# Two products against the same weights joined into one of 512 columns in the late feed-forward blocks of a decoder layer

## Chip, cores and metric

The kernel runs on one core of one Trainium2 chip. The metric is the device time of one execution in microseconds (us). The kernel before was run three times; the median is 517.9 us (517.75 to 518.09).

## What is computed

The reference is one decoder layer over 256 tokens of 1024 channels, in float32. Two token mixers (a gated linear recurrence and a block-sparse attention) read the same input, are projected, gated, merged and normalised. What the change touches comes behind that: the feed-forward part, with D_FF = 2816.

```python
x = layer_norm(DN_ALPHA * x + mixed, ln1_w, ln1_b)      # called x1 in the kernel
h = jnp.einsum('bsd,df->bsf', x, w_ffn_in)              # 1024 -> 2 * 2816
h_gate, h_up = jnp.split(h, 2, axis=-1)
y = jnp.einsum('bsf,fd->bsd', jax.nn.silu(h_gate) * h_up, w_ffn_down)
return layer_norm(DN_ALPHA * x + y, ln2_w, ln2_b)
```

## The kernel before, in words

**Three products for one.** TensorE is fed with a rounded format (fp32r). To keep float32 accuracy each operand is split into leading bits and a rest: `split` (L135) lets ScalarE copy the value into the rounded format (L136) and VectorE subtract that copy from the value (L137). A product a·w is then the sum of three: ah·wh, al·wh and ah·wl, accumulated in the same PSUM area.

**Weights.** `plan` (L71) lists all weight tiles of 1 MB in the order of their use. `stage` (L143) loads one tile over SyncE's queue (SP, L158) into one of three raw buffers (pool wraw), ScalarE casts it to wh (L159) and VectorE subtracts to get wl (L161); wh and wl have four buffers each (pools whi and wlo). `fetch` (L165) hands out the next tile and keeps up to three more staged ahead.

**Blocks of the feed-forward part.** A tile of w_ffn_in has 8 steps k (128 input channels each) of 256 output columns, so two blocks f of 128 features. `feat_pair` (L205) takes one tile, one PSUM bank `[128, 2, 256]` of the pool mm, and calls `feat_steps` (L213) for f = 0 and 1. There the weights are the stationary operand, 128 x 128, and the 256 tokens are the moving one: for each k three products of 256 columns (L217: wh with the leading bits, L218: wh with the rest, L219: wl with the leading bits). Each product loads its own weights into the array.

**x1** is normalised token half by token half (`norm1`), transposed on TensorE (L595) and split into x1h and x1l, two tiles of 8 KB per partition from the pool big (12 slots). The first EARLY = 4 feature blocks are done another way (`FfnEarly`, L599): there x1 is stationary and the weights move. The order of the instructions of TensorE, VectorE and ScalarE is written out by hand up to L665 (`manual_schedule`); behind it a scheduler with a cost model orders the instructions of each engine at build time, in program order where nothing speaks for another.

**The late loop**, j = 4, 6, ... 20 (L670 to L677), nine iterations: a gate tile (name fg) and an up tile (fu), each with `feat_pair`; ScalarE takes Silu of the gate bank (L674), VectorE multiplies with the up bank (L675), and `split` writes two blocks of ah and al, which the down projection reads.

**The down projection** (L679 to L691) has five PSUM parts: two of 512 columns for the first token half, and 512, 256 and 256 for the second. The first four come from the pool aux, the last from mm. Each pool has four banks. aux is not used in the late loop before, except for the last transposes of the early blocks (tile fet, L628).

Of the kernel before, what the change touches and what calls it, by code (L numbers as in the profile page):

```python
# [10 lines left out]
F32 = mybir.dt.float32  # L11
F32R = mybir.dt.float32r
U32 = mybir.dt.uint32
AF = mybir.ActivationFunctionType
# [3 lines left out]
P = 128  # L18
T = 256
NT = T // P  # L20
D = 1024
KC = D // P
# [88 lines left out]
def hybrid_layer_kernel(ctx: ExitStack, tc, x, xT, vecs, wts, ln1_w, ln1_b, ln2_w, ln2_b, consts, out):  # L111
    nc = tc.nc
# [6 lines left out]
    sm = pool("sm", 2)  # L119
    klp = pool("klp", 1)  # L120
    mm = pool("mm", 4, space=PSUM)
    aux = pool("aux", 4, space=PSUM)

    def slot(name, dt=F32):
        return big.tile([P, 2048], dt, tag="s8", name=name)

    def r32(ap):
        return ap.bitcast(F32)


    loads = plan()
# [3 lines left out]
    def split(dst_h, dst_l, src):  # L135
        nc.scalar.copy(dst_h, src)  # L136
        nc.vector.tensor_sub(dst_l, src, r32(dst_h))  # L137
# [5 lines left out]
    def stage(pieces=None, eng=nc.vector):  # L143
        i = state["next"]
        if i >= len(loads):
            return
        state["next"] += 1
        _, _, k, _, _, held = loads[i]
        src = wts[i].rearrange("p (k c) -> p k c", k=k)
        view = lambda z: z.rearrange("p (k c) -> p k c", k=k)  # L150
        raw = view(wraw.tile([P, 2048], F32, tag="raw", name=f"raw{i}"))
        if held:
            h, l = view(slot(f"wh{i}", F32R)), view(slot(f"wl{i}", F32R))
        else:
            h = view(whi.tile([P, 2048], F32R, tag="h", name=f"wh{i}"))
            l = view(wlo.tile([P, 2048], F32R, tag="l", name=f"wl{i}"))
        for ks in ks_of(pieces or (k,)):
            nc.sync.dma_start(raw[:, ks, :], src[:, ks, :])  # L158
            nc.scalar.copy(h[:, ks, :], raw[:, ks, :])  # L159
            yield  # L160
            eng.tensor_sub(l[:, ks, :], raw[:, ks, :], r32(h[:, ks, :]))  # L161
            yield
        ready.append((h, l))

    def fetch(ahead=LOOKAHEAD):  # L165
        while state["next"] < len(loads) and len(ready) < 1 + ahead:
            list(stage())
        return ready.pop(0)
# [36 lines left out]
    def feat_pair(name, ah=None, al=None):  # L205
        ah, al = (xTh, xTl) if ah is None else (ah, al)
        wh, wl = fetch()
        ps = mm.tile([P, 2, T], F32, tag="mm", name=name)
        for f in range(2):
            feat_steps(ps[:, f, :], wh, wl, f, ah, al, range(KC))  # L210
        return ps

    def feat_steps(ps, wh, wl, f, ah, al, ks, k0=0):  # L213
        wcol = slice(f * P, (f + 1) * P)
        for k in ks:
            kk = k0 + k
            nc.tensor.matmul(ps, wh[:, k, wcol], ah[:, kk, :], start=(kk == 0), stop=False)  # L217
            nc.tensor.matmul(ps, wh[:, k, wcol], al[:, kk, :], start=False, stop=False)  # L218
            nc.tensor.matmul(ps, wl[:, k, wcol], ah[:, kk, :], start=False, stop=(kk == KC - 1))  # L219
# [62 lines left out]
    for j in range(2, 4):  # L282
        ps = feat_pair(f"hf{j}")
# [4 lines left out]
    for j in range(4):  # L288
        ps = feat_pair(f"hq{j}")
        sg = sm.tile([P, 2, T], F32, tag="sg", name=f"sgq{j}")  # L290
# [23 lines left out]
    def hgrn_steps():  # L314
# [5 lines left out]
        nc.vector.tensor_mul(kq, flat(Kt), flat(Qg))  # L320
        nc.scalar.copy(kqh, kq)
        nc.vector.tensor_sub(kql, kq, r32(kqh))
        for g in range(4):
            ps = aux.tile([P, 4, P], F32, tag="aux", name=f"sd{g}")
# [73 lines left out]
    class Steps:  # L398
        def __init__(self):
            self.gens = []  # L400
# [21 lines left out]
    for j in range(4):  # L422
        ps = feat_pair(f"hg{j}")
        sg = sm.tile([P, 2, T], F32, tag="sg", name=f"sgg{j}")
# [90 lines left out]
    for j in range(4):  # L515
        side.step()
        ps = feat_pair(f"za{j}", yah, yal)
# [5 lines left out]
    for j in range(4):  # L523
        ps = feat_pair(f"zb{j}", ybh, ybl)
# [45 lines left out]
    def row_parts(name, widths, n0=0):  # L570
        parts = []
        for i, (p, w) in enumerate(widths):
            parts.append((p.tile([P, w], F32, tag="aux" if p is aux else "mm", name=f"{name}{i}"), n0))
            n0 += w
        return parts
# [2 lines left out]
    nc.gpsimd.dma_start(xr, x.rearrange("(t p) d -> p t d", p=P))  # L578
    wb1 = bcast("wb1", ln1_w, ln1_b)
    x1 = slot("x1").rearrange("p (t d) -> p t d", t=NT)  # L580
    x1h = slot("x1h", F32R).rearrange("p (k t) -> p k t", k=KC)
    x1l = slot("x1l", F32R).rearrange("p (k t) -> p k t", k=KC)
    ah = [slot(f"ah{i}", F32R).rearrange("p (k t) -> p k t", k=KC) for i in range(3)]
    al = [slot(f"al{i}", F32R).rearrange("p (k t) -> p k t", k=KC) for i in range(3)]

# [3 lines left out]
    def norm1_transpose(t):  # L589
        ts = slice(t * P, (t + 1) * P)  # L590
        for g in range(2):
            ps = mm.tile([P, 4, P], F32, tag="mm", name=f"x1t{t}{g}")
            for a in range(4):
                k = 4 * g + a
                nc.tensor.transpose(ps[:, a, :], x1[:, t, k * P:(k + 1) * P], ident)  # L595
            ks = slice(4 * g, 4 * g + 4)
            split(x1h[:, ks, ts], x1l[:, ks, ts], ps)

    class FfnEarly:  # L599

# [6 lines left out]
        def product(self, i, w):  # L607
            (wh, wl), ps, ts = w, self.ps[:, i, :], self.ts
            for k in range(KC):
                nc.tensor.matmul(ps, x1h[:, k, ts], wh[:, k, :], start=(k == 0), stop=False)  # L610
                nc.tensor.matmul(ps, x1l[:, k, ts], wh[:, k, :], start=False, stop=False)
                nc.tensor.matmul(ps, x1h[:, k, ts], wl[:, k, :], start=False, stop=(k == KC - 1))

        def gate(self):
            self.product(0, self.wg)
# [17 lines left out]
    pss = [row_parts(f"wo{t}", [(aux, 512)] * 2) for t in range(NT)]  # L633
    wb2 = bcast("wb2", ln2_w, ln2_b)
    with tc.manual_schedule(engines={ET.PE, ET.DVE, ET.Activation}):
# [5 lines left out]
        for q in range(4):  # L641
            if q == 3:
                norm1_transpose(0)
            rows_pass(pss[1], lhs, 1, tiles[q:q + 1], KC)
            if q < 2:
                prefetch(1)
# [5 lines left out]
        e[0][0].silu()  # L652
        e[0][1].gate()
        norm1_transpose(1)
        prefetch(2)
        e[0][1].up()
# [10 lines left out]
    e[1][1].transpose()  # L667


    for j in range(EARLY, NF, 2):  # L670
        pg = feat_pair(f"fg{j}", x1h, x1l)
        pu = feat_pair(f"fu{j}", x1h, x1l)
        sg = sm.tile([P, 2, T], F32, tag="sg", name=f"sf{j}")
        nc.scalar.activation(sg, pg, AF.Silu)  # L674
        nc.vector.tensor_mul(sg, sg, pu)  # L675
        i, k = divmod(j, KC)
        split(ah[i][:, k:k + 2, :], al[i][:, k:k + 2, :], sg)  # L677

    pss = [row_parts("wd0", [(aux, 512)] * 2), row_parts("wd1", [(aux, 512), (aux, 256), (mm, 256)])]  # L679
    lhs = (lambda kk: ah[kk // KC][:, kk % KC, :], lambda kk: al[kk // KC][:, kk % KC, :])  # L680
# [43 lines left out]
```

## Time and profile before

| | before |
|---|---|
| median of 3 runs | 517.9 us (517.75 to 518.09) |
| profiled execution, its own time | 517.71 us |
| its span, first to last instruction | 515.7 us |
| granted TensorE clock, mean | 0.997 |
| late loop (first fg product to first wd product) | 343.55 to 447.51 us |
| down projection to the last product | 447.51 to 508.29 us |

The profile comes from one execution. Engines are called PE (TensorE's products), PEld (its weight loads), DVE (VectorE), ACT (ScalarE), POOL (GpSimd) and SP (SyncE). A row of the timeline has the start in us from the span's start, the duration in us, engine, line, operation, output<-inputs by the program's tile names, and, in brackets, how long the engine was idle before and what ended that. A row of the groups has the count, the total busy time, the mean ns of one, and the idle time before them with its releaser. A row of the waits has who waited for whom, the total in us, the times, and the longest.

### The profile page before, as it was taken

Reading aid. Unit: us, or ns where it says so; the run is one execution under the profiler, and the core shown is the slowest. Engines: PE = TensorE matmul, PEld = TensorE weight load, DVE = VectorE, ACT = ScalarE, POOL = GpSimd, SP = SyncE. Lnnn points to the kernel's source line nnn. Section 1 sums busy time; section 2 is a strip of 40 time slices with the busy share of each in tenths; the row PEclk is TensorE's granted clock in tenths of the full one; section 3 lists DMA queues with packets and bytes.
Section 4 is the critical chain, followed back from the end, with each engine's and each line's share of the span. In section 5 each row is a group of like instructions: output and inputs, shape, how many; then the busy total and the mean of one; then the engine's idle time right before and its main releaser. Section 6 shows DMA issues by size and latency. Waiting matters only on the chain.

```text
span 515.7 us, 8629 instructions
## 1 busy us (share of the span) xinstructions
PE 506.5 (98%) x3728; PEld 484.8 (94%) x3728; DVE 327.2 (63%) x351; ACT 236.1 (46%) x267; POOL 39.9 (8%) x33
## 2 busy tenths in 40 slices
PE   8999999999999999999999999999999999999994
PEld 7999889999999998998999988999999999988884
DVE  4677799997575444775772899555445454543436
ACT  5695355444354455656442553543443344324300
POOL 0000000000110162353010001000000000000000
PEclk9999999999999999999999999999999999999998
DMA  7988453343424555444575475055554455456002
GB/s 236 354 305 323 167 186 142 128 151 131 164 83 165 168 188 216 165 163 160 179 247 232 163 275 215 5 213 198 192 209 167 165 186 210 174 168 203 39 1 81
DMA packets 15573, 91.73 MB, mean 178 GB/s; under 512 B 1840, under 2 KB 2864, under 8 KB 5552
## 3 DMA queue, kind: packets, MB, share of 16 engines
q1 hardware_dynamic: 14688, 88.04, 47.5%
q0 software_dynamic: 848, 3.15, 1.9%
q8 instruction: 29, 0.48, 0.4%
q14 instruction: 8, 0.07, 0.0%
HBM read 90.13 MB, written 1.05 MB: 177 GB/s over the span
## 4 chain that ended last, share of the span: by engine, by line
PE 98%; DMA 1%; DVE 1%; issue 0%; DVEq 0%; ACT 0%; SPq 0%
PE wd L547 4%; PE wd L546 4%; PE wd L548 4%; PE fu L217 3%; PE fg L218 3%; PE fg L217 3%; PE fg L219 3%; PE fu L218 3%; PE fu L219 3%; PE sc L343 3%; PE hf L219 2%; PE hf L217 2%; PE hf L218 2%; PE mk L219 1%; PE hq L219 1%; PE hq L218 1%
## 5 line engine op out<-in xcount | busy, mean ns | idle before, releaser
L161 DVE TENSOR_TENSOR wl<-raw,wh 128x2048 fp32r<-128x2048 f32 (+2 forms) x88 | 186.6, 2122 | 123.1 <-ACT wh L159 122.7
L159 ACT CAST wh<-raw 128x2048 fp32r<-128x2048 f32 (+2 forms) x88 | 155.8, 1772 | 186.1 <-issue 50.3
L217 PE MATMUL fg<-x1h,wh 128*128 128x256 f32 x144 | 40.8, 284 | 0.0
L217 PE MATMUL fu<-x1h,wh 128*128 128x256 f32 x144 | 40.8, 284 | 0.0
L218 PE MATMUL fg<-x1l,wh 128*128 128x256 f32 x144 | 40.8, 283 | 0.0
L219 PE MATMUL fg<-x1h,wl 128*128 128x256 f32 x144 | 40.8, 283 | 0.0
L218 PE MATMUL fu<-x1l,wh 128*128 128x256 f32 x144 | 40.7, 283 | 0.0
L219 PE MATMUL fu<-x1h,wl 128*128 128x256 f32 x144 | 40.7, 283 | 0.0
L547 PE MATMUL wd<-wl,ah 128*128 128x512 f32 (+1 forms) x110 | 38.2, 348 | 0.0
L546 PE MATMUL wd<-wh,ah 128*128 128x512 f32 (+1 forms) x110 | 38.2, 347 | 0.0
L548 PE MATMUL wd<-wh,al 128*128 128x512 f32 (+1 forms) x110 | 38.1, 347 | 0.0
L218 PEld LDWEIGHTS fg<-x1l,wh 128*128 128x128 f32 x144 | 27.6, 192 | 0.0
L219 PEld LDWEIGHTS fg<-x1h,wl 128*128 128x128 f32 x144 | 27.6, 192 | 0.0
L217 PEld LDWEIGHTS fg<-x1h,wh 128*128 128x128 f32 x144 | 27.6, 192 | 0.0
L218 PEld LDWEIGHTS fu<-x1l,wh 128*128 128x128 f32 x144 | 27.6, 192 | 0.0
L219 PEld LDWEIGHTS fu<-x1h,wl 128*128 128x128 f32 x144 | 27.6, 192 | 0.0
L217 PEld LDWEIGHTS fu<-x1h,wh 128*128 128x128 f32 x144 | 27.6, 192 | 0.0
L546 PEld LDWEIGHTS wd<-wh,ah 128*128 128x128 f32 x110 | 20.8, 189 | 2.7
L548 PEld LDWEIGHTS wd<-wh,al 128*128 128x128 f32 x110 | 20.8, 189 | 2.7
L547 PEld LDWEIGHTS wd<-wl,ah 128*128 128x128 f32 x110 | 20.8, 189 | 2.6
L217 PE MATMUL hf<-xTh,wh 128*128 128x256 f32 x64 | 19.3, 301 | 1.0 <-ACT wh L159 1.0
L219 PE MATMUL hf<-xTh,wl 128*128 128x256 f32 x64 | 19.3, 302 | 0.0
(218 smaller groups left out, 1436.5 us busy)
## 6 DMA issues: line engine op xcount, KB each, us to landing
raw<-in_wts_dram SPq DMA_DIRECT2D x78, 1024.0 KB, 4.8
raw<-in_wts_dram SPq DMA_DIRECT2D x8, 256.0 KB, 5.0
xTr<-in_xT_dram SPq DMA_DIRECT2D x8, 128.0 KB, 4.7
raw<-in_wts_dram SPq DMA_DIRECT2D x2, 512.0 KB, 7.0
xr<-in_x_dram POOLq DMA_DIRECT2D x1, 1024.0 KB, 5.4
wb<-in_ln_w_dram POOLq DMA_DIRECT2D x2, 512.0 KB, 5.7
wb<-in_ln_b_dram POOLq DMA_DIRECT2D x2, 512.0 KB, 7.4
out_dram<-y SPq DMA_DIRECT2D x4, 256.0 KB, 2.1
```

The source lines that it names most:

```text
L159: nc.scalar.copy(h[:, ks, :], raw[:, ks, :])
L161: eng.tensor_sub(l[:, ks, :], raw[:, ks, :], r32(h[:, ks, :]))
L217: nc.tensor.matmul(ps, wh[:, k, wcol], ah[:, kk, :], start=(kk == 0), stop=False)
L218: nc.tensor.matmul(ps, wh[:, k, wcol], al[:, kk, :], start=False, stop=False)
L219: nc.tensor.matmul(ps, wl[:, k, wcol], ah[:, kk, :], start=False, stop=(kk == KC - 1))
L343: nc.tensor.matmul(ps[:, a, :], KL[:, h, :], later(Qt, n, h, 1), start=True, stop=True)
L546: nc.tensor.matmul(ps, lh(kk)[:, ts], wh[:, k, ns], start=(kk == 0), stop=False)
L547: nc.tensor.matmul(ps, lh(kk)[:, ts], wl[:, k, ns], start=False, stop=False)
L548: nc.tensor.matmul(ps, ll(kk)[:, ts], wh[:, k, ns], start=False, stop=(kk == ktot - 1))
```

## The change

The two parts of x1 move into a common layout. `Pair` holds two tiles of the same size as x1h and x1l before; each has four steps k, and for each k the 256 tokens of the leading bits and then the 256 of the rest, so that both lie next to each other: 512 columns. Transposes, splits and `FfnEarly` address the parts through it.

In the late loop `wide_pair` takes the place of `feat_pair`. For each block f it takes a PSUM bank of its own, `[128, 2, 256]`. For each k one product of 512 columns (wh with both parts) fills both halves of the bank, and one product of 256 (wl with the leading bits) adds to the first half. Gate blocks use the pool mm, up blocks the pool aux. ScalarE then copies the second half of each bank to SBUF and VectorE adds the first half to it. Silu, the product of gate and up, and the split work on these sums, which lie in a new tile `room` of the pool big, with two places for gate and two for up, used in turn. The down projection and everything else are as before.

```diff
+    class Pair:
+        def __init__(self, name):
+            self.parts = [slot(f"{name}{i}", F32R).rearrange("p (k u t) -> p k u t", k=KC // 2, u=2)
+                          for i in range(2)]
+        def __getitem__(self, key):
+            u, ks, ts = key
...
+            return self.parts[i][:, ks, u, ts]
+        def both(self, k):
+            i, k = divmod(k, KC // 2)
+            return self.parts[i][:, k, :, :]
...
-    x1h = slot("x1h", F32R).rearrange("p (k t) -> p k t", k=KC)
-    x1l = slot("x1l", F32R).rearrange("p (k t) -> p k t", k=KC)
+    x1p = Pair("x1p")
...
-            split(x1h[:, ks, ts], x1l[:, ks, ts], ps)
+            split(x1p[0, ks, ts], x1p[1, ks, ts], ps)
...
+    def wide_pair(name, p, tag):
+        wh, wl = fetch()
+        pss = []
+        for f in range(2):
+            ps = p.tile([P, 2, T], F32, tag=tag, name=f"{name}{f}")
+            wcol = slice(f * P, (f + 1) * P)
+            for k in range(KC):
+                nc.tensor.matmul(ps, wh[:, k, wcol], x1p.both(k), start=(k == 0), stop=False)
+                nc.tensor.matmul(ps[:, 0, :], wl[:, k, wcol], x1p[0, k, slice(0, T)],
+                                 start=False, stop=(k == KC - 1))
+            pss.append(ps)
+        return pss
+
+    room = slot("room").rearrange("p (i f t) -> p i f t", i=4, f=2)
     for j in range(EARLY, NF, 2):
-        pg = feat_pair(f"fg{j}", x1h, x1l)
-        pu = feat_pair(f"fu{j}", x1h, x1l)
-        sg = sm.tile([P, 2, T], F32, tag="sg", name=f"sf{j}")
-        nc.scalar.activation(sg, pg, AF.Silu)
-        nc.vector.tensor_mul(sg, sg, pu)
+        n = j // 2 % 2
+        sums = []
+        for i, (nm, p, tag) in enumerate([("g", mm, "mm"), ("u", aux, "aux")]):
+            pss = wide_pair(f"f{nm}{j}", p, tag)
+            s = room[:, 2 * i + n, :, :]
+            for f, ps in enumerate(pss):
+                nc.scalar.copy(s[:, f, :], ps[:, 1, :])
+                nc.vector.tensor_add(s[:, f, :], ps[:, 0, :], s[:, f, :])
+            if i == 0:
+                nc.scalar.activation(s, s, AF.Silu)
+            sums.append(s)
+        nc.vector.tensor_mul(sums[0], sums[0], sums[1])
         i, k = divmod(j, KC)
-        split(ah[i][:, k:k + 2, :], al[i][:, k:k + 2, :], sg)
+        split(ah[i][:, k:k + 2, :], al[i][:, k:k + 2, :], sums[0])
```

More of the change, by code (lines that the diff above doesn't have):

```diff
@@ L128, in r32 @@
         return ap.bitcast(F32)
+    class Pair:
[4 more added lines that the diff above has]
+            u, ks, ts = key
+            if isinstance(ks, int):
+                i, ks = divmod(ks, KC // 2)
+            else:
+                i, k0 = divmod(ks.start, KC // 2)
+                ks = slice(k0, k0 + ks.stop - ks.start)
+            return self.parts[i][:, ks, u, ts]
+        def both(self, k):
+            i, k = divmod(k, KC // 2)
+            return self.parts[i][:, k, :, :]
     loads = plan()
@@ L609, in product @@
             for k in range(KC):
-                nc.tensor.matmul(ps, x1h[:, k, ts], wh[:, k, :], start=(k == 0), stop=False)
-                nc.tensor.matmul(ps, x1l[:, k, ts], wh[:, k, :], start=False, stop=False)
-                nc.tensor.matmul(ps, x1h[:, k, ts], wl[:, k, :], start=False, stop=(k == KC - 1))
+                nc.tensor.matmul(ps, x1p[0, k, ts], wh[:, k, :], start=(k == 0), stop=False)
+                nc.tensor.matmul(ps, x1p[1, k, ts], wh[:, k, :], start=False, stop=False)
+                nc.tensor.matmul(ps, x1p[0, k, ts], wl[:, k, :], start=False, stop=(k == KC - 1))
         def gate(self):
```

## The prediction, made before the changed kernel was run

> **What bounds the kernel now.** I read the page first (busy shares, chain), then the waits of TensorE, then the timeline inside the late FFN loop.
>
> ```profile
> span 515.7 us, 8629 instructions
> PE 506.5 (98%) x3728; PEld 484.8 (94%) x3728; DVE 327.2 (63%) x351; ACT 236.1 (46%) x267; POOL 39.9 (8%) x33
> PE 98%; DMA 1%; DVE 1%; issue 0%; DVEq 0%; ACT 0%; SPq 0%
> ```
>
> TensorE holds 98% of the chain that ended last; VectorE and ScalarE have a third and a half of the span free. The waits of TensorE alone:
>
> ```profile
> PE warm L264 <- DVE half L265: 1.1, 1, 1.1
> PE hf L217 <- ACT wh L159: 1.0, 1, 1.0
> ```
>
> Both lie at the start of the kernel. In the late FFN loop TensorE waits for nothing. One iteration of that loop (one j), in the table by stretches (us, then busy time and instructions of PE, PEld, DVE, ACT, POOL; clock; DMA share; GB/s):
>
> ```profile
> 354.93:366.45 11.52, 11.52 (x98) 11.52 (x98) 5.87 (x4) 4.82 (x4) 0.00 (x0) 1.00 0.47 180
> ```
>
> The reader sees a full TensorE at clock 1.00, VectorE busy 5.87 and ScalarE 4.82 of 11.52 us. So the time of this stage is the number of its products times their spacing, and what shortens the products shortens the kernel, unless something new makes TensorE wait.
>
> The page's mean of 284 ns for a product is its latency, with the next product already running. The spacing is read from starts. From the first product of block fg of j=20 to the first of fu there are 48 products of 256 columns:
>
> ```profile
> 435.99 0.28 PE L217 MATMUL fg<-x1h,wh 128*128 128x256 f32 x1
> 441.75 0.28 PE L217 MATMUL fu<-x1h,wh 128*128 128x256 f32 x1
> ```
>
> 5.76 / 48 = 0.1200 us each. Products of 512 columns, which the output projection already issues (63 between these two):
>
> ```profile
> 300.51 0.39 PE L546 MATMUL wo<-wh,mTh 128*128 128x512 f32 x1
> 314.79 0.39 PE L546 MATMUL wo<-wh,mTh 128*128 128x512 f32 x1
> ```
>
> 14.28 / 63 = 0.2267 us each. Twice the columns cost 0.2267, not 0.2400: a product of either length carries about 13.3 ns that do not grow with its columns.
>
> **The change, part by part.**
>
> *Products.* In each of the 9 iterations (j = 4 to 20) there are 4 blocks (g and u, f = 0 and 1) of 8 steps k. Each step had three products of 256; it now has one of 512 (wh with both parts of x1) and one of 256 (wl). Removed are 288 products and weight loads: 288 x 13.3 ns = 3.84 us, if the pair costs 0.2267 + 0.1200 = 0.3467. An iteration then takes 32 x 0.3467 = 11.09 us instead of 11.52.
>
> A strict alternation of 512 and 256 is nowhere in the trace of before, only single transitions. From 256 to 512 (start of the down projection), and from 512 to 256 (its third part):
>
> ```profile
> 447.51 0.40 PE L546 MATMUL wd<-wh,ah 128*128 128x512 f32 x1
> ...
> 447.98 0.39 PE L548 MATMUL wd<-wh,al 128*128 128x512 f32 x1
> ```
>
> ```profile
> 451.62 0.28 PE L546 MATMUL wd<-wh,ah 128*128 128x256 f32 x1
> ...
> 451.85 0.28 PE L548 MATMUL wd<-wh,al 128*128 128x256 f32 x1
> ```
>
> The first two products of 512 after short ones take 0.47 / 2 = 0.235 each, 8 ns over the steady spacing; the first two of 256 after long ones 0.23 / 2 = 0.115 each, 5 ns under it. Bounds for the pair: 0.2267 + 0.115 = 0.342 (the short one keeps its gain: saves 18 ns, 5.3 us in all) and 0.235 + 0.120 = 0.355 (only the long one's loss: saves 5 ns, 1.4 us). An alternation has both transitions in every pair, and they nearly cancel, so I take the steady value, 0.3467 and **-3.84 us**.
>
> *Evacuation.* Before, per j: one Silu from PSUM, one product of g and u, one split. Now each of the 4 blocks gets a ScalarE copy of 256 columns from PSUM and a VectorE addition of 256 from PSUM; Silu, product and split stay, over 512 columns of SBUF. The nearest rows:
>
> ```profile
> L136 ACT CAST ybh<-po 128x256 fp32r<-128x256 f32 x8 | 2.9, 366 | 7.6 <-PE po L490 7.6
> L623 DVE TENSOR_TENSOR se<-se,fe x4: 410/412/420, 326.8 to 347.7; 128x256 f32<-128x256 f32 x4
> L675 DVE TENSOR_TENSOR sf<-sf,fu 128x512 f32<-128x512 f32 x9 | 6.2, 687 | 14.9 <-PE fu L219 14.9
> L674 ACT ACTIVATE sf<-fg 128x512 f32<-128x512 f32 x9 | 5.3, 593 | 0.0
> ```
>
> ScalarE gains 4 x 0.37 = 1.5 us per j, to 6.3 of 11.09; VectorE 4 x 0.41 = 1.6, to 7.5 (68%). Silu and the product I leave at 0.59 and 0.69, although they no longer read PSUM. Both engines stay under TensorE, which hides all of this: price nothing. A copy between Silus could need a change of table:
>
> ```profile
> 325.08 1.28 ACT L622 ACT_TABLE_LOAD   x1 [7.90 <-PE fe L612]
> ```
>
> After this load casts and Silus alternate in the whole stage with no other one; if the copies brought two loads per j, that is 2.6 us more of ScalarE, 8.9 of 11.09, still hidden.
>
> *What is queued behind it.* Copies and additions stand in the same in-order queues as the casts and subtractions that prepare the weights, and the transfers on SP's queue wait for those subtractions:
>
> ```profile
> L159 ACT CAST wh<-raw 128x2048 fp32r<-128x2048 f32 x78 | 148.7, 1909 | 179.3 <-issue 50.3 <-PE fu L218 23.2 <-PE wd L548 21.7
> L161 DVE TENSOR_TENSOR wl<-raw,wh 128x2048 fp32r<-128x2048 f32 x78 | 178.6, 2292 | 116.5 <-ACT wh L159 116.3
> SPq L158 <- DVE wl L161: 376.1, 67, 15.9
> raw<-in_wts_dram SPq DMA_DIRECT2D x78, 1024.0 KB, 4.8
> ```
>
> A cast starts when TensorE has finished with the tile whose buffer it takes (four buffers), so it is needed three tiles later: 3 x 5.54 = 16.6 us, against 1.91 + 2.29 = 4.2 us of work. Some 12 us of delay are free. A transfer, with three raw buffers, has 16.6 us against 4.8. Four copies or additions of 0.4 us in front use little of this.
>
> *PSUM banks.* A tile of weights took one bank of mm; now g takes two of mm and u two of aux per j, so a bank comes back after two iterations, 22 us: no wait inside the loop. At the end there is one. The down projection uses all four aux banks, the last of them for the first part of 256 (at 451.62, 4.1 us after its start at 447.51), and that bank now holds u, f = 1 of j = 20, whose products end just before 447.51. Its copy and addition meet this in the queues:
>
> ```profile
> 447.59 1.91 ACT L159 CAST wh<-raw 128x2048 fp32r<-128x2048 f32 x1 [3.32 <-PE fu L218]
> 449.40 0.61 ACT L136 CAST ah<-sf 128x512 fp32r<-128x512 f32 x1
> 449.53 2.29 DVE L161 TENSOR_TENSOR wl<-raw,wh 128x2048 fp32r<-128x2048 f32 x1 [1.06 <-ACT wh L159]
> 451.74 0.68 DVE L137 TENSOR_TENSOR al<-sf,ah 128x512 fp32r<-128x512 f32 x1
> ```
>
> If the cast goes first, the copy runs at 449.40 to 449.77, behind the start of the subtraction, and the addition at 451.74 to 452.15: the bank is free 0.55 us late. If the copy goes first, or the scheduler moves the mm part ahead of the aux part (0.72 us of work), it costs nothing. The scheduler does move products: the last transposes of the early blocks stand ahead of this loop in the program and were issued inside the second tile's products, at 350.9:
>
> ```profile
> L628 PE MATMUL fet<-cst,se x8: 270/272/273, 337.2 to 350.9; 128*128 128x128 f32 x8
> ```
>
> I take half, **+0.3 us**. The last block's ah and al are late by the same 2 us or so, but are read only at the end of the down projection.
>
> *Layout of x1.* The two parts now lie side by side in one tile. Same instructions, same sizes. If the dependences took interleaved pieces for overlapping, the early products after the second transpose would wait for VectorE:
>
> ```profile
> 327.88 0.87 PE x1t L595 x8
> 328.97 1.29 DVE L137 TENSOR_TENSOR x1l<-x1t,x1h 128x512 fp32r<-128x512 f32 x2 [1.76 <-ACT x1h L136]
> ```
>
> that is from 328.75 to 330.26, 1.5 us at most. Before, the two token halves interleave in the same way and TensorE did not wait there, so I take nothing. The slot "room" is a new 8 KB tile of the big pool; at its first use the held weights, mTh, mTl, xr and wb1 are done with: nothing.
>
> **Sum**: -3.84 + 0.3 = -3.5 us. The profiled execution took 517.71 us around its span of 515.7, so 514.2; the median of the three runs, 517.9, lies 0.2 above it. Forecast **514.4 us**.
>
> **Rivals.**
>
> *The alternation keeps the overhead* (pair at 0.355). For it: the row of 0.235. Against: 0.115 in the other rows. Saves 1.4, less 0.3 to 0.55 for the bank: 516.8 to 517.0. The Trainium skill, page "TensorE: Matmul & The Clock Gate", section "Back-to-back issue gap", gives the spacing of a warm matmul as its columns over 2.4 GHz plus some 2.5 ns. By that figure a merged product saves 2.5 ns, an estimate of 0.7 us in all and 517.2 us. The trace disagrees: 0.1200 and 0.2267 leave 13.3 ns, not 2.5.
>
> *The load of the next weights is exposed* (slower). Place: the 512 product behind a short one, when its load has had too little time. The row for that is the moving of long products among transposes:
>
> ```profile
> 235.24 0.48 PE L236 MATMUL mv<-wh,xTh 128*128 128x512 f32 x1
> 235.56 0.40 PE L237 MATMUL mv<-wh,xTl 128*128 128x512 f32 x1
> ```
>
> There a 512 product takes 0.32. A pair of 0.32 + 0.12 is 0.08 over the old 0.36: 288 x 0.08 = +23 us, 541. It decides from a pair of 0.360 on. Against it: the short product is as long as those of before, which hide a load each at 0.12; and no 512 row behind a 256 one is above 0.24.
>
> *An engine in order holds TensorE up in each iteration.* A block's addition sits behind a cast that waits, and the weights come late. To undo 3.84 us takes 0.43 us per j; that needs delays beyond the 12 us of slack. Time between 516 and 519.
>
> *The change does not do what it says*: the merged product split again by the build would give 517.9. The output projection's 512 columns are one instruction each, so hardly.
>
> **Chances.** The forecast's case (pair 0.342 to 0.352, bank 0 to 0.55) has 0.80: all faster by over 0.2%, which is about what a measurement of this kernel can tell from no change, 1.04 us. The kept overhead has 0.10, half of it faster, half within 0.2%. The exposed load has 0.04, slower. Engines in order 0.05: 0.01 faster, 0.02 same, 0.02 slower. A split product 0.01, same. Together: faster 0.86, same 0.08, slower 0.06. The range: below, the pair at 0.342 and no wait at the bank, 517.9 - 5.3 = 512.6, less 0.2 for rows of two decimals, 512.4; above, the pair at 0.353 (-2.0) with the bank (+0.55), 516.5, and a little of the next case, 516.7.
>
> **What would show it.** Right: pairs starting 0.347 us apart; an iteration of 11.09; TensorE full over the loop and the down projection starting 3.8 us earlier; VectorE near 7.5 and ScalarE near 6.3 us per j; at most one new wait of TensorE, for the addition's bank in the down projection. Wrong: a pair of 0.355 or more, waits of TensorE for wh or wl inside the loop, or waits at the early blocks for x1's parts.

## The result, and the profile after

The changed kernel takes 514.13 us (median of 4 runs, 513.28 to 514.50), the kernel before 518.0 us on the same chip (4 runs, 517.75 to 518.72). The ratio is 0.9928, with a 95% interval of 0.9917 to 0.9940: 0.72% faster. The forecast was 514.4 us, in a range of 512.4 to 516.7. The profiled execution of after took 513.88 us around a span of 511.8.

The page of after, its busy shares, its chain and the two groups that take the place of L217 to L219 in the late loop:

```profile
span 511.8 us, 8120 instructions
PE 501.4 (98%) x3440; PEld 467.3 (91%) x3440; DVE 338.5 (66%) x387; ACT 249.1 (49%) x303; POOL 39.9 (8%) x33
PE 94%; DMA 3%; DVE 1%; SPq 1%; ACT 0%; issue 0%; DVEq 0%
...
L698 PE MATMUL fg<-x1p,wh 128*128 128x512 f32 x144 | 50.4, 392 | 0.0
...
L699 PE MATMUL fg<-x1p,wl 128*128 128x256 f32 x144 | 40.3, 280 | 0.0
```

There are 288 products fewer (3728 to 3440), and TensorE still has the chain; the 3% of DMA are transfers at the start of the chain, before 21.3 us. The whole list of TensorE's waits has no entry from the late loop or the down projection:

```profile
PE hf L239 <- DVE wl L181: 1.3, 3, 0.8
PE warm L284 <- DVE half L285: 1.1, 1, 1.1
PE hf L237 <- ACT wh L179: 0.9, 1, 0.9
```

One iteration in the table by stretches (us, then busy time and instructions of PE, PEld, DVE, ACT, POOL; clock; DMA share; GB/s):

```profile
377.09:388.19 11.10, 11.10 (x67) 9.79 (x66) 7.12 (x9) 6.25 (x8) 0.00 (x0) 1.00 0.52 192
```

TensorE is full at clock 1.00; VectorE has gone from 5.87 to 7.12, ScalarE from 4.82 to 6.25. The spacing is in the timeline; ten pairs lie between the first and the last of these rows:

```profile
399.63 0.39 PE L698 MATMUL fg<-x1p,wh 128*128 128x512 f32 x1
399.86 0.28 PE L699 MATMUL fg<-x1p,wl 128*128 128x256 f32 x1
399.97 0.39 PE L698 MATMUL fg<-x1p,wh 128*128 128x512 f32 x1
...
403.09 0.39 PE L698 MATMUL fg<-x1p,wh 128*128 128x512 f32 x1
```

3.46 / 10 = 0.346 us for a pair, as the steady spacings of before said (0.3467). The reader should also see how it is shared out: the long product takes 0.23, the short one 0.12 or a little under. The starts of the loop and of the down projection are:

```profile
343.50 0.48 PE L698 MATMUL fg<-x1p,wh 128*128 128x512 f32 x1
...
443.65 0.39 PE L566 MATMUL wd<-wh,ah 128*128 128x512 f32 x1
```

The loop lasts 100.15 us; before it lasted 447.51 - 343.55 = 103.96. The difference, 3.81 us, is nearly all of the 3.9 by which the span is shorter.

### The profile page after: what moved, and what is told of

It is laid out like the page before. It is cut to its first block, busy times and chain, and to the rows that moved or that the text cites. A ratio compares the mean times of both kernels' runs of the same rounds, so it can differ in the third digit from the quotient of the medians.

```text
span 511.8 us, 8120 instructions
## 1 busy us (share of the span) xinstructions
PE 501.4 (98%) x3440; PEld 467.3 (91%) x3440; DVE 338.5 (66%) x387; ACT 249.1 (49%) x303; POOL 39.9 (8%) x33
## 4 chain that ended last, share of the span: by engine, by line
PE 94%; DMA 3%; DVE 1%; SPq 1%; ACT 0%; issue 0%; DVEq 0%
PE fg L698 6%; PE fu L698 6%; PE wd L567 4%; PE wd L566 4%; PE wd L568 4%; PE fu L699 3%; PE fg L699 3%; DMA raw<-in_wts_dram 3%; PE sc L363 3%; PE mk L239 2%; PE hq L239 2%; PE hq L238 2%; PE hq L237 2%; PE zb L239 2%; PE za L239 2%; PE mk L238 2%
## 5 line engine op out<-in xcount | busy, mean ns | idle before, releaser
L698 PE MATMUL fg<-x1p,wh 128*128 128x512 f32 x144 | 50.4, 392 | 0.0
L698 PE MATMUL fu<-x1p,wh 128*128 128x512 f32 x144 | 50.4, 392 | 0.0
L699 PE MATMUL fg<-x1p,wl 128*128 128x256 f32 x144 | 40.3, 280 | 0.0
L699 PE MATMUL fu<-x1p,wl 128*128 128x256 f32 x144 | 40.3, 280 | 0.0
L698 PEld LDWEIGHTS fg<-x1p,wh 128*128 128x128 f32 x144 | 26.9, 187 | 5.9
L698 PEld LDWEIGHTS fu<-x1p,wh 128*128 128x128 f32 x144 | 26.9, 187 | 5.9
L699 PEld LDWEIGHTS fg<-x1p,wl 128*128 128x128 f32 x144 | 27.2, 189 | 0.0
L699 PEld LDWEIGHTS fu<-x1p,wl 128*128 128x128 f32 x144 | 27.2, 189 | 0.0
L239 PE MATMUL za<-yah,wl 128*128 128x256 f32 x64 | 18.5, 288 | 0.0
L238 PE MATMUL za<-yal,wh 128*128 128x256 f32 x64 | 18.4, 288 | 0.0
```

Source lines behind the costliest of these rows:

```text
L698: nc.tensor.matmul(ps, wh[:, k, wcol], x1p.both(k), start=(k == 0), stop=False)
L699: nc.tensor.matmul(ps[:, 0, :], wl[:, k, wcol], x1p[0, k, slice(0, T)], start=False, stop=(k == KC - 1))
```

## Experiments

The theory to test: each product carries about 13.3 ns beside its columns; the gain is the number of products removed times this, and nothing that the change adds is paid. The rivals: the gain comes from banks, layout or order; or it belongs to the alternation of long and short. The loop's length, from the first product fg to the first product wd in each run's timeline, tells more than the time of a whole run:

| kernel | time, us (runs) | ratio to before, 95% | loop, us |
|---|---|---|---|
| before | 518.0 (4) | | 103.96 |
| after | 514.13 (4) | 0.9917 to 0.9940 | 100.15 |
| e1_three | 517.23 (11) | 0.9987 to 1.0004 | 103.96 |
| e2_half | 516.61 (10) | 0.9967 to 0.9986 | 102.97 |
| e2b_gates | 515.84 (6) | 0.9954 to 0.9979 | 102.55 |
| e3_apart | 514.34 (6) | 0.9931 to 0.9961 | 100.85 |
| e4_evac | 513.65 (5) | 0.9912 to 0.9936 | 100.15 |
| e10_entry | 515.51 (8) | 0.9956 to 0.9978 | 102.00 |

### All but the merging (e1_three)

```diff
-                nc.tensor.matmul(ps, wh[:, k, wcol], x1p.both(k), start=(k == 0), stop=False)
+                for u in range(2):
+                    nc.tensor.matmul(ps[:, u, :], wh[:, k, wcol], x1p[u, k, slice(0, T)],
+                                     start=(k == 0 and u == 0), stop=False)
```

> The changed kernel with its layout of x1, its banks and its evacuation, but each k again with three products of 256 columns (leading bits and rest of x1 apart). Theory (the gain is 288 products fewer at 13.3 ns each, and copies and additions are hidden): the gain is gone, 517.9 us, and the late loop lasts 9 x 11.52 us again. Rival (the gain, or part of it, comes from the two banks per tile, the layout or another order): clearly under 517, towards 514.

The loop has its old 103.96 us and the time is that of the kernel before, within the interval. Layout, two banks per tile, copies and additions neither give nor cost anything. The gain is the merging alone.

### More evacuation than needed (e4_evac)

```diff
                 nc.scalar.copy(s[:, f, :], ps[:, 1, :])
+                nc.scalar.copy(s[:, f, :], ps[:, 1, :])
+                nc.vector.tensor_add(s[:, f, :], ps[:, 0, :], s[:, f, :])
+                nc.scalar.copy(s[:, f, :], ps[:, 1, :])
                 nc.vector.tensor_add(s[:, f, :], ps[:, 0, :], s[:, f, :])
```

> The changed kernel with the evacuation of each block made longer without need: three copies and two additions instead of one of each, one waiting for the other. ScalarE then has about 6.3 + 3.0 = 9.3 and VectorE 7.3 + 1.7 = 9.0 us of work in an iteration of 11.09. Theory (evacuation lies beside the products and the banks come back after two iterations): the same as the changed kernel within its spread, 514.1, at most 0.5 more at the start of the down projection, where a bank is needed soon. Rival (the evacuation sits in the queue of the casts and already costs part of the gain): over 515.5, with waits of TensorE for weights or banks in the loop.

An iteration of this kernel:

```profile
388.19:399.28 11.09, 11.09 (x66) 9.79 (x65) 8.44 (x13) 8.43 (x17) 0.00 (x0) 1.00 0.50 184
```

VectorE and ScalarE now work 8.4 us each of 11.09 (less than the 9.0 and 9.3 that were expected), and the loop is as long as in the changed kernel. The cover is real, and is not yet used up at 76%.

### The same products, sorted (e3_apart)

```diff
             for k in range(KC):
                 nc.tensor.matmul(ps, wh[:, k, wcol], x1p.both(k), start=(k == 0), stop=False)
+            for k in range(KC):
                 nc.tensor.matmul(ps[:, 0, :], wl[:, k, wcol], x1p[0, k, slice(0, T)],
```

> As many products of each length as in the changed kernel, but per block first all eight of 512 columns and then all eight of 256. Theory (a fixed part per product, whatever its neighbours): 8 x 0.2267 + 8 x 0.1200 per block, the same 2.773 us, so 514.1 us, plus what one transition per block costs: by the start of the down projection in the kernel before (long products behind short ones 8, 8 and then fewer ns late, some 0.02 us in all) 36 x 0.02 = 0.7 us, 514.8 us. Rival (the alternation itself is what is cheap, the fixed part is smaller in it): over 516.

The loop is 100.85, 0.70 us longer, which is the 36 switches at 0.02 that were written down. So the fixed part does not need the alternation, and a switch from a run of short products to long ones has its own price.

### Half the merging, two ways (e2_half, e2b_gates)

```diff
+                if k < KC // 2:
                     nc.tensor.matmul(ps, wh[:, k, wcol], x1p.both(k), start=(k == 0), stop=False)
+                else:
+                    for u in range(2):
+                        nc.tensor.matmul(ps[:, u, :], wh[:, k, wcol], x1p[u, k, slice(0, T)],
+                                         start=False, stop=False)
```

> The merged product for k = 0 to 3 only, three products of 256 for k = 4 to 7: 144 products fewer instead of 288. Theory (a fixed part per product): half the gain, 517.9 - 1.92 = 516.0 us, an iteration of 11.31 us. Rival (the gain belongs to the alternation of long and short, and runs of equal products behave otherwise, with single transitions of 0.235 or 0.115): a loop that differs from 9 x 11.31 by the transitions, 36 blocks x about 0.02 = 0.7 us, so 515.3 or 516.7.

Half the products gave a quarter of the gain: the loop is 0.99 us shorter, not 1.92. The second arrangement merges all steps of the gate blocks and none of the up blocks (`if p is mm:` in place of `if k < KC // 2:`):

> Half the merging in another arrangement: all eight steps of the gate blocks merged, the up blocks with three products of 256, so again 144 products fewer, but one switch from a run of short products to merged ones per iteration (9 in all) instead of one per block (36). Theory (13.3 ns per product, and some 0.025 us for each such switch, which is what kept the other half from its full share): the late loop lasts 103.96 - 1.92 + 0.23 = 102.3 us, against 102.97 there, and the time is 516.2 us. Rival (half the products are worth only a quarter of the gain for another reason): the loop lasts 103.0 again, 516.6 us.

Between the two expectations: 1.41 us shorter, 102.55. Switches at 0.025 do not explain it. The timeline of e2_half does; here are the first three pairs of a block and the start of the fourth:

```profile
389.00 0.40 PE L699 MATMUL fg<-x1p,wh 128*128 128x512 f32 x1
389.23 0.28 PE L704 MATMUL fg<-x1p,wl 128*128 128x256 f32 x1
389.35 0.40 PE L699 MATMUL fg<-x1p,wh 128*128 128x512 f32 x1
389.59 0.28 PE L704 MATMUL fg<-x1p,wl 128*128 128x256 f32 x1
389.71 0.40 PE L699 MATMUL fg<-x1p,wh 128*128 128x512 f32 x1
389.94 0.28 PE L704 MATMUL fg<-x1p,wl 128*128 128x256 f32 x1
390.06 0.40 PE L699 MATMUL fg<-x1p,wh 128*128 128x512 f32 x1
```

The pairs take 0.35, 0.36, 0.35, and over three of them 1.06 / 3 = 0.3533, not 0.3467. Of the 144 pairs of this run 136 are like that; 136 x 0.0067 = 0.91 us is the missing half, 0.93. In e2b_gates 73 of the 144 pairs are like that (all 16 of the gate tiles of j = 8, 12, 16 and 20, and nine of j = 6), and nearly all the others have 0.347: 73 x 0.0067 = 0.49, against 0.51 missing. So the pair has two patterns in this loop. What stands directly in front does not decide between them alone: from j = 8 on, each gate tile follows an up tile of 48 short products, and the tiles have the pattern of 0.353 and that of 0.347 in turn. Here are the first products of the gate tile and of the up tile behind it, for j = 8 and j = 10:

```profile
366.04 0.40 PE L699 MATMUL fg<-x1p,wh 128*128 128x512 f32 x1
371.69 0.28 PE L702 MATMUL fu<-x1p,wh 128*128 128x256 f32 x1
...
377.46 0.40 PE L699 MATMUL fg<-x1p,wh 128*128 128x512 f32 x1
383.01 0.28 PE L702 MATMUL fu<-x1p,wh 128*128 128x256 f32 x1
```

The 16 pairs take 5.65 us in the first and 5.55 in the second: 0.353 and 0.347 for a pair.

### Where the pattern comes from (e10_entry)

```diff
+                if name == "fg6" and f == 0:
+                    for u in range(2):
+                        nc.tensor.matmul(ps[:, u, :], wh[:, k, wcol], x1p[u, k, slice(0, T)],
+                                         start=(k == 0 and u == 0), stop=False)
+                else:
                     nc.tensor.matmul(ps, wh[:, k, wcol], x1p.both(k), start=(k == 0), stop=False)
```

> The changed kernel with a single block, gate j = 6, f = 0, done with three products of 256; everything else stays merged. The runs before showed two patterns of a pair that each go on once begun: 0.3467 us behind a group of 128-column products (as the loop of the changed kernel begins), 0.3533 behind a run of 256-column products (all pairs of the half-merged run, 64 in a row in the q and k stage). Theory (the pattern is set by what stands in front and is kept): all 248 pairs behind that block take 0.3533, so the loop is longer than the changed kernel's 100.16 by 248 x 0.0067 + 8 x 0.0133 = 1.8 us, 101.9, and the time is 515.9 us. Rival (the slow pattern dies out within a block or two, and only the eight products more are paid): the loop lasts 100.3 us, 514.2 us.

One block of short products, eight more in all, and the pairs behind it are in the other pattern to the end. Here are rows over 40 us behind the block (nine pairs from first to last):

```profile
400.13 0.40 PE L703 MATMUL fg<-x1p,wh 128*128 128x512 f32 x1
400.37 0.28 PE L704 MATMUL fg<-x1p,wl 128*128 128x256 f32 x1
400.49 0.40 PE L703 MATMUL fg<-x1p,wh 128*128 128x512 f32 x1
400.73 0.28 PE L704 MATMUL fg<-x1p,wl 128*128 128x256 f32 x1
...
403.31 0.40 PE L703 MATMUL fg<-x1p,wh 128*128 128x512 f32 x1
```

3.18 / 9 = 0.353. The loop lasts 102.00 us: 1.85 more than in the changed kernel, where 1.8 was expected, and the time is 515.51. The build had put 14 of the block's 24 short products ahead of the up tile of j = 4 and ten behind it, so 16 + 248 = 264 pairs stand behind the first of them, and all but the one directly behind two transposes have the long pattern: 264 x 0.0067 + 8 x 0.0133 = 1.87. The two transposes lie between the 14 products and the up tile, as they lie ahead of the up tile of the changed kernel, and they did not bring the short pattern back here. In e2_half they did: there short products also stand ahead of the transposes, and the third and fourth pair behind them take 0.347. So one block of short products can change the pattern for the rest of the loop, as was expected; but this case, with e2b_gates beside it, shows no rule that says which pattern comes.

### The bank at the start of the down projection (e5_order, e5b_order)

```diff
-        rows_pass(pss[0], lhs, 0, tiles[-1:], NF)
-        if q < NF // 2 - HOLD_DOWN:
-            rows_pass(pss[1], lhs, 1, tiles[-1:], NF)
+        if q == 0:
+            with tc.manual_schedule(engines={ET.PE}):
+                rows_pass(pss[0], lhs, 0, tiles[-1:], NF)
+                rows_pass(pss[1], lhs, 1, tiles[-1:], NF)
+            continue
...
```

> The changed kernel with the products of the down projection's first tile kept on TensorE in the order of the program (two parts of 512, then 512, 256 from aux, 256 from mm), where the build had put the mm part ahead. Theory (the last aux bank comes back some 4.7 us after the loop, behind a cast on ScalarE and a subtraction on VectorE, and the changed kernel escaped only by the order): TensorE waits once for the addition from fu, 0.5 to 0.7 us, and the time is 514.1 + 0.6 = 514.7 us. Rival (the bank is back in time in any order): no wait, 514.1 us.

No wait, 513.21 us (4 runs). But this run did not test what it was meant to: the build put the long products of the second tile ahead of the part in question. So the whole loop was fixed in the program's order (e5b_order, the same `manual_schedule` around `for q in range(NF // 2)`):

> The changed kernel with all products of the down projection's loop in the order of the program, so that nothing can be put ahead of the part that needs the last aux bank. Theory (that bank is free at about 4.7 us after the loop's end, and needed at 4.1): one wait of TensorE for an addition of fu, 0.5 to 0.7 us, and 514.1 + 0.6 = 514.7 us. Rival (no wait, the bank is not late): 514.1 us.

514.60 us (4 runs, ratio 0.9931 to 0.9958). In its timeline VectorE's subtraction for the weights comes first, then the addition, and TensorE waits for it:

```profile
445.60 2.29 DVE L181 TENSOR_TENSOR wl<-raw,wh 128x2048 fp32r<-128x2048 f32 x1 [1.99 <-ACT wh L179]
447.81 0.42 DVE L713 TENSOR_TENSOR room<-fu,room 128x256 f32<-128x256 f32 x1
```

```profile
447.47 0.39 PE L568 MATMUL wd<-wh,al 128*128 128x512 f32 x1
448.28 0.38 PE L566 MATMUL wd<-wh,ah 128*128 128x256 f32 x1 [0.42 <-DVE room L713]
```

Between these starts lie 0.81 us instead of 0.23: 0.58 us lost, where 0.55 had been worked out. The first product behind the wait takes 0.22 instead of 0.12 as well, and the down projection is 0.68 us longer than in the changed kernel (61.48 against 60.80, first to last start). The bank really is late; the rows show it, the medians of 514.60 and 514.13 alone would not. The changed kernel does not pay, because the build put the part from mm and the long products of the second tile ahead: the addition ends at 448.31, and the next products of 256 columns start at 452.59.

### The same merging elsewhere (e6_gates, e7_more, e8_qk, e9_q)

The kernel has the same three products in nine more stages. `wide_pair` gets the activations as an argument, both banks of a tile come from mm, and the consumers read the sum:

```diff
-            ps = feat_pair(f"{name}{j}")
+            pss = wide_pair(f"{name}{j}", mm, "mm", xp)
             for f in range(2):
                 c = 2 * j + f
-                nc.scalar.activation(g[:, c, :], ps[:, f, :], AF.Sigmoid, bias=bg[:, b0 + c:b0 + c + 1])
+                evacuate(g[:, c, :], pss[f])       # copy of one half, addition of the other
+                nc.scalar.activation(g[:, c, :], g[:, c, :], AF.Sigmoid, bias=bg[:, b0 + c:b0 + c + 1])
```

> The changed kernel with the same merging in four more stages (two gate stages and the two branch projections, 16 tiles of weights, 256 products fewer), both banks of a tile from mm, the activations' parts side by side too. Theory (13.3 ns per product, evacuation hidden): 514.1 - 3.4 = 510.7 us. Rival (in these stages products of other work stand between, only two tiles fit into mm, and VectorE is at two thirds of its time: waits for banks, or switches between lengths at 0.02 each, eat the gain): 512 to 514 us, with waits of TensorE for additions.

528.23 us (ratio 1.0172 to 1.0224): slower than the kernel before, and worse than the rival said. The first gate stage gained its price: from the first gb to the first ga it takes 32.03 us (109.34 to 141.36) against 32.83 in the changed kernel. The second lost far more. There the recurrence goes through ScalarE, VectorE and GpSimd, and TensorE does products of ga meanwhile: in the changed kernel 61 of them (7.4 us) lie between the recurrence's last products (tile o) and the transposes (tile ot) that need its result, here 18 (3.4 us). TensorE's waits in this stage, and two stretches of it:

```profile
PE ot L440 <- DVE on L432: 4.6, 2, 2.3
PE ga L258 <- DVE ga L267: 1.9, 1, 1.9
```

```profile
158.00:165.00 7.00, 2.31 (x9) 1.71 (x10) 5.96 (x9) 2.19 (x7) 0.63 (x1) 0.66 0.37 150
165.00:172.00 7.00, 7.00 (x27) 5.96 (x27) 1.59 (x4) 2.61 (x7) 0.00 (x0) 0.61 0.01 2
```

TensorE is busy for 2.31 of the first 7 us. Two of the waits are for the recurrence (VectorE's on). The third is for a bank, as the rival said:

```profile
162.90 0.62 ACT L164 CAST yap<-ya 128x512 fp32r<-128x512 f32 x1 [4.81 <-DVE ya L442]
163.43 1.19 ACT L266 COPY ga<-ga 128x256 f32<-128x256 f32 x4
164.63 0.80 PE L258 MATMUL ga<-xp,wh 128*128 128x512 f32 x1 [1.85 <-DVE ga L267]
```

The 64 products of ga issued by 156.00 fill all four banks of mm. The copies that begin to free them stand on ScalarE behind a cast that waits 4.81 us for the recurrence, so no fifth block of ga can start before them. Whether copies in another place, or other banks, would avoid this was not tried.

The clock in these rows is a mean. It was granted in full up to 160.27 us and by half for 10.24 us from there:

```profile
156.27:160.27 4.00, 0.41 (x2) 0.20 (x2) 2.94 (x5) 1.82 (x1) 1.98 (x2) 1.00 0.06 23
160.27:170.51 10.24, 7.42 (x24) 6.15 (x25) 4.86 (x10) 4.17 (x11) 0.00 (x0) 0.50 0.26 104
```

At half the clock the pairs behind the waits take 0.64 us instead of 0.347. The Trainium skill, page "TensorE: Matmul & The Clock Gate", section "What's actually happening", says that TensorE falls to half its rate after an idle window of some 3.4 us. The trace agrees with the half; in the 4.00 us ahead of the fall TensorE did two transposes of 0.41 us together and nothing else. No run here shows the length of the window.

From the first ga to the first mk this stage takes 37.2 us (141.36 to 178.53) against 27.4 in the changed kernel (141.83 to 169.28): 9.7 us more, where all 256 products together could give 3.4. Another 5.5 us are lost from the first za to the first fe (81.42 against 75.92), where TensorE has waits of 0.9 to 1.8 us for ScalarE and VectorE.

> As the one with four more stages, and the recurrence's output gate and the attention's q and k as well: 28 tiles beyond the changed kernel, 448 products fewer. Theory: 514.1 - 6.0 = 508.1 us. Rival (q and k go on through a chain of ScalarE, VectorE and GpSimd that the sums now lengthen, and the scores wait for it): 510 to 513 us, with waits of TensorE at the scores or for banks.

527.91 us (1.0165 to 1.0229). The late loop begins at 355.68 against 358.24 in e6_gates, 2.56 us earlier: as much as the price of 192 products, and the next expectation rests on that. The agreement is chance: 1.18 us of it lies ahead of the first hq (30.31 against 31.49), where the two kernels do the same products, the stretch from the first mk to the first za is 2.53 shorter, and the one from there to the first fe 2.18 longer. The next run kept only those stages:

> The changed kernel with the merging in the stages of the recurrence's output gate and of the attention's q and k (12 tiles, 192 products fewer), without the gate and branch stages whose merging let TensorE run out of work. Theory (13.3 ns per product where TensorE has work all along; the two runs with more stages differ by exactly this in the start of the late loop): 514.1 - 2.56 = 511.6 us. Rival (in these stages the sums' way through ScalarE, VectorE and GpSimd makes the scores or the recurrence wait): 513 us or more, with waits of TensorE there.

513.40 us (5 runs, 0.9909 to 0.9934): not distinguishable from the changed kernel, 514.13. From the first mk to the first za it is 1.95 us shorter (241.32 - 169.43 against 243.11 - 169.28), and the output gate stage 0.77. But from the first za to the first fe it is 2.23 us longer (319.47 - 241.32 against 319.03 - 243.11), and there stands a wait that the changed kernel has not:

```profile
PE wo L600 <- DVE mTl L165: 0.6, 2, 0.4
```

TensorE reaches the output projection before VectorE has all of what that reads (mTl). About half of the 2.23 is in the output projection, where this wait lies; for the rest, in the branch stages, the runs show no single cause.

> As the one before, and the recurrence's q stage as well (4 tiles, 64 products, 0.85 us more), where VectorE is already busy for 85% of the time. Theory: 510.7 us if VectorE keeps up. Rival (VectorE is the bound there, and the additions push back what it prepares): 511.6 or more, with weights or the recurrence late.

514.04 us (5 runs, 0.9917 to 0.9942), again the same. The q stage itself (first hq to first hi) became 0.44 us shorter instead of 0.85, as nearly all of its pairs have the long pattern, and the stage behind it is 0.49 longer (first hi to first sd).

No version tried is clearly better than the changed kernel.

## Why the prediction was right

- **The bound.** TensorE was and is full in the loop, so products times spacing is the time.
- **Products, -3.84.** Measured in the loop: -3.81. The steady spacings of 256 and 512 columns, read from before, add up to the pair. e1_three shows that nothing else gave it. The pattern is not a matter of one execution: in the seven other kernels whose late loop has the same products in the same order (e4, e5, e5b, e6 to e9), it lasts 100.15 or 100.16.
- **Evacuation and queues, nothing.** Shown by e4_evac, with more than twice the work. The estimate of 6.3 for ScalarE met 6.25; that of 7.5 for VectorE was a little high in this stretch (7.12).
- **The bank, +0.3.** Half of a price that is paid whole or not at all. It was not paid; e5b_order shows the whole of it, 0.58. The sum without it, 514.06, would have been nearer to 514.13, but runs of after differ by over 1 us and do not tell the two sums apart.
- **Layout of x1, room, tables, nothing.** No wait shows at the early blocks, and e1_three has the layout and the tile at no cost.
- **The rival "the alternation keeps the overhead".** It was given 0.10 and a pair of 0.355. Such a pattern exists, 0.3533, and e10_entry shows it in this very loop: 515.51 us, still inside the range. The prediction had a transition of 0.235 in one place and one of 0.115 in another, and let them cancel, as if an alternation had only one pattern. That the forecast's pair came, and not the other, was luck: nothing in the prediction's argument would have told which one comes. The formula of the Trainium skill beside this rival (page "TensorE: Matmul & The Clock Gate", section "Back-to-back issue gap") is given there for a single product in isolation, and this loop is a stream of loads and products; the 13.3 ns from the trace decided.
- **The slower rival.** Behind a pair of transposes the next long product took 0.31 us instead of 0.23, twice in all; behind a short product never (0.24 at most).

## What to carry to other kernels

Where TensorE is the bound, read the spacing of its products from their starts, not their duration, for each length: what doesn't grow with the columns is what fewer, longer products save. The gain arrives only where the added evacuation lies under the products and the banks come back in time: the same edit that gave 3.8 us in a stage of pure products cost 14 us net in four other stages, most of it in one where the copies that free the banks stood behind a chain on other engines and TensorE stood idle. A bank that comes back late can be hidden by the order in which the build happens to place the work; fix the order once to see its price.

## What the runs showed of the hardware that was not expected

- A stream of 512- and 256-column products with new weights for each has two spacings that keep going: 0.3467 us for a pair in the changed kernel, in 263 pairs in a row, and 0.3533 in e10_entry, in 248. A block of 24 short products in front was enough to change from one to the other. It is no rule: in e2b_gates the two alternate behind equal runs of 48 short products. What inside TensorE makes the two patterns was not tried and stays open.
- A switch from a run of 256-column products to a run of 512 costs some 0.02 us (0.70 us for 36 in e3_apart).
- In e6_gates 4.00 us in which TensorE did no more than two transposes (0.41 us) went ahead of a fall of the granted clock from 1.00 to 0.50, which lasted 10.24 us. No single wait was longer than 2.3 us. e7_more has the same fall, again for 10.24 us.
